# A two-mixer block on one core: the delta-rule merges eight turns later, with more zero products around them

## The chip, the cores and the metric

The kernel runs on one core of one Trainium2 chip. A core has a matmul engine (TensorE, PE in the profile, with its weight loads as PEld), a vector engine (DVE), an activation engine (ACT), a general-purpose engine (POOL), DMA queues fed from SyncE (SP), an on-chip memory (SBUF) and the matmul's accumulators (PSUM). Every engine works through its own list of instructions in order and meets the others at semaphores. The metric is the device time of one execution in microseconds.

## The reference

Three blocks follow each other on 256 tokens of width 1024, in float32. The first holds gated feed-forwards, a Mamba-2 mixer and a windowed attention. The last holds two mixers that read the same normalised input and a feed-forward with 16384 small experts. The change lies in the two mixers, which the reference computes so:

```
q = rms_norm(c_q, g_cq) @ w_uq          # 8 heads of 96
k_nope = rms_norm(c_kv) @ w_uk ; v = rms_norm(c_kv) @ w_uv
o = softmax(mask(q k^T * scale)) v ; o = rms_norm(o, g_attn_out)      # mixer 1

def rwkv7_step(state, inp):             # mixer 2, 256 steps, 8 heads of 64
    sk = einsum('bhij,bhj->bhi', state, kk_t)
    state = state * w_t - sk * (kk_t * a_t) + v_t * k_t
    y = einsum('bhij,bhj->bhi', state, r_t)
y = (group_norm(y) * ln_x_w + ln_x_b + bonus) * g
h = h + concat(o, y) @ w_o
```

## The kernel before, in words

Products of float32 matrices are made of three products of rounded halves: `mm3` (L153 to L155) multiplies low by high, high by low and high by high. Weights arrive by DMA as `wraw`; L93 (ACT) rounds them to `whi` and L99 (DVE or POOL) leaves the rest as `wlo`.

All of both mixers stands in `mixers`, as two generators that `run` steps in turn, one step of each per turn; a scheduler then sets every engine's list from the order in which this code records instructions. `weave(gens, lag)` starts one more generator every `lag` turns and steps all that live.

`rwkv` solves the delta rule in chunks of 64 steps. For each of four groups n of (chunk, head) pairs `gram` makes the triangular matrices; `base` inverts their 16 by 16 blocks by substitution on DVE (L1061, L1062) and writes X (L1074 on DVE, L1076 on ACT). Six empty turns follow (L1215). Then `merge(n)` joins the blocks at two levels: a zero product by `K.warm` (L77: a 256-column product of a zero tile with itself, into the bank that the next product overwrites), X times Lo on PE (L1088), a mask on DVE (L1091), another zero product, a product with Wt (L1097), a subtraction on DVE (L1099). After that `recur` runs four chunks c in order: state times AR (L1121, not for c = 0), MV (L1123), X times MV (L1129), VS (L1131 on ACT, L1132 on DVE), the state's update (L1139, L1153 to L1156) and the outputs `py` (L1147, L1148). After c = 1 and after c = 3 one half of the tokens is finished (`finish`): copies (L1170, ACT), mean and square (L1171 to L1176, DVE and ACT), nine small DVE operations of an inverse root (L168 to L176), a gate product (L1180, PE), two passes on POOL (L1184, L1185), four on DVE (L1186 to L1189), transposes (L1195, PE) and the split into bhi (L1202, ACT) and blo (L1203, DVE).

`mla` is the attention: `queries(m)`, m = 0 to 3, multiplies cqh and cql with 18 products each; `by_token` makes keys and values (kb); sums of squares are L1267; eight heads follow. Their output po is squared (L1410, ACT), summed (L1411, DVE), scaled by an inverse root (small DVE operations L168 to L176 again, named rsm) into ay (L1419, DVE), transposed (L1426, PE) and split into ahi (L1432, ACT) and alo (L1433, DVE). The output projection has 96 products of ahi and alo, then, once both generators have ended, 96 of bhi and blo; L264 (DVE) adds to h.

In the changed kernel every line past L1214 has one more in its number (L1426 is L1427).

Of the kernel before, what the change touches and what calls it, by code (L numbers as in the profile page):

```python
# [23 lines left out]
def weave(gens, lag=1):  # L24

    live, t = [], 0
    gens = list(gens)
    while gens or live:
        if gens and t % lag == 0:
            live.append(gens.pop(0))  # L30
        for g in list(live):
            if next(g, live) is live:
                live.remove(g)
        t += 1
        yield
# [765 lines left out]
def mixers(K, h, P, W, pool):  # L801
# [83 lines left out]
    def prep_k(m):  # L885
        ns = slice(2 * m, 2 * m + 2)
        ps = K.bank()
        for j in range(2):
            for st in range(2):
                for e, p in enumerate(halves):  # L890
                    K.bcast(kks, st, 4 * m + 2 * j + e, 64, ps[p, j * T + st * 128:j * T + (st + 1) * 128])
        kkn = tile_([128, 2, T], F32, name="kkn", tag="kkn")
        for j in range(2):
            n = 2 * m + j
            V.scalar_tensor_tensor(kkn[:, j], kT[:, n], P["kk"][:, n:n + 1], ps[:, j * T:(j + 1) * T], OP.mult, OP.mult)
        dp = Dp[:, 8 * m:8 * m + 8].rearrange("p (n c) j -> p n c j", c=4)
        di = Di[:, 8 * m:8 * m + 8].rearrange("p (n c) j -> p n c j", c=4)
        V.tensor_tensor(AR[:, ns, :, 0:64], chunked(kkn), dp[:, :, :, 0:64], OP.mult)
        V.tensor_mul(kkn, kkn, ra[:, ns])
        for j in range(2):  # L900
            n = 2 * m + j
            A.activation(ra[:, n], ra[:, n], AF.Identity, scale=P["ka"][:, n:n + 1], bias=ka1[:, n:n + 1])
        for e, p in enumerate(halves):
            V.tensor_tensor(BK[p, ns, :, 64 * e:64 * e + 64], chunked(kkn)[p], di[p], OP.mult)
        V.tensor_mul(kT[:, ns], ra[:, ns], kT[:, ns])
        for e, p in enumerate(halves):
            V.tensor_tensor(BK[p, ns, :, 64 - 64 * e:128 - 64 * e], chunked(kT[:, ns])[p], di[p], OP.mult)

    def prep_r(m):
        ns = slice(2 * m, 2 * m + 2)  # L910
        dp = Dp[:, 8 * m:8 * m + 8].rearrange("p (n c) j -> p n c j", c=4)
        V.tensor_tensor(AR[:, ns, :, 64:128], chunked(rT[:, ns]), dp[:, :, :, 1:65], OP.mult)
        for j in range(2):
            n = 2 * m + j
            V.scalar_tensor_tensor(rT[:, n], rT[:, n], P["rk"][:, n:n + 1], kT[:, n], OP.mult, OP.mult)
# [34 lines left out]
    ps = pair(2)  # L950
# [4 lines left out]
    ps = pair(3)  # L955
    kk_norm(1, sqs)
    shifted(ps, 3, 6, [rT[:, 0], rT[:, 1]])
    ps = pair(4)
# [64 lines left out]
    def gram(n):  # L1023

        s = slice(4 * n, 4 * n + 4)
        pgs = [K.bank(), K.bank()]
        for c in range(4):
            for e, p in enumerate(halves):
                TE.matmul(pgs[e][:, c * 128:(c + 1) * 128], BK[p, n, c], AR[p, n, c], start=True, stop=True)
        for e in range(2):  # L1030
            V.tensor_tensor(GM[e][:, s], pgs[e].rearrange("p (a b) -> p a b", b=128), gm, OP.mult)
        yield
        pts, pl = [K.bank(), K.bank()], K.bank()
        for c in range(4):
            for e, p in enumerate(halves):
                TE.transpose(pts[e][:, c * 64:c * 64 + 64], BK[p, n, c], ident[p, p])
        for c in range(4):
            for e, p in enumerate(halves):
                TE.matmul(pl[p, c * 64:c * 64 + 64], AR[p, n, c, 0:64], BK[p, n, c, 64 * e:64 * e + 64], start=True, stop=True)
        for e, hb, q in quads:  # L1040
            V.tensor_tensor(D16[q, s], GM[e][q, s, 32 * hb:32 * hb + 32], b16[q], OP.mult)
        yield
        for e in range(2):
            A.activation(BKt[:, n, e], b4(pts[e]), AF.Copy)
        A.activation(Lo[:, s], b4(pl), AF.Copy)
        yield

    def base():

        Tr = tile_([128, 16, 32], F32, name="Tr", tag="ry", bufs=2)  # L1050
        UX = tile_([128, 2, 256], F32, name="UX", tag="rsq")
        U, Y = (UX[:, i].rearrange("p (c i) -> p c i", i=16) for i in range(2))
        G.memset(UX[:, 1], 0.0)
        G.memset(UX[:, 1, 0:256:17], 1.0)
        dv = D16.rearrange("p b (s j) -> p j s b", s=2)
        V.transpose(Tr, dv)
        yield
        V.tensor_tensor(U, Tr[:, :, 0:16], Tr[:, :, 16:32], OP.add)
        for j in range(15, 0, -1):
            t = tile_([128, 64], F32, name="bt", tag="bt", bufs=2)[:, :j * (16 - j)].rearrange("p (c i) -> p c i", i=j)  # L1060
            V.tensor_tensor(t, U[:, j:j + 1, 0:j].to_broadcast([128, 16 - j, j]), Y[:, j:, j:j + 1].to_broadcast([128, 16 - j, j]), OP.mult)  # L1061
            V.tensor_tensor(Y[:, j:, 0:j], Y[:, j:, 0:j], t, OP.subtract)  # L1062
            if j % 4 == 1:
                yield
        m = P["b16"][:, 32:34]
        A.activation(Tr[:, :, 0:16], Y, AF.Copy, scale=m[:, 0:1])
        V.tensor_scalar(Tr[:, :, 16:32], Y, m[:, 1:2], None, OP.mult)
        yield
        V.transpose(dv, Tr)
        yield  # L1070
        for e, hb, q in quads:
            dst = X[q, :, 32 * hb:32 * hb + 32]
            if e:
                V.tensor_copy(dst, D16[q])  # L1074
            else:
                A.activation(dst, D16[q], AF.Copy)  # L1076
        yield

    def merge(n):

        s = slice(4 * n, 4 * n + 4)
        for lv in range(2):
            V.transpose(XT[:, s], X[:, s])
            ps = K.bank()
            K.warm(ps, 1)
            for c in range(4):
                for p in halves:
                    TE.matmul(ps[p, c * 64:c * 64 + 64], Lo[p, 4 * n + c], X[p, 4 * n + c], start=True, stop=True)  # L1088
            yield
            Wt = tile_([128, 4, 64], F32, name="Wt", tag="Wt", bufs=2)  # L1090
            V.tensor_tensor(Wt, b4(ps), um(lv), OP.mult)  # L1091
            yield
            ps = K.bank()
            K.warm(ps, 1)
            for c in range(4):
                for p in halves:
                    TE.matmul(ps[p, c * 64:c * 64 + 64], XT[p, 4 * n + c], Wt[p, c], start=True, stop=True)  # L1097
            yield
            V.tensor_tensor(X[:, s], X[:, s], b4(ps), OP.subtract)  # L1099
            yield  # L1100
# [106 lines left out]
    def rwkv():  # L1207
        for i in range(4):
            yield
            if i == 0:  # L1210
                prep_k(1)
                prep_r(1)
        yield from weave((gram(n) for n in range(4)), 2)
        yield from base()  # L1214
        for _ in range(6):  # L1215
            yield
        yield from weave((merge(n) for n in range(4)), 1)
        while MV is None:
            yield
        r = recur()  # L1220
        for _ in r:
            if todo and next(todo[0], todo) is todo:
                todo.pop(0)
            yield
        while todo:
            if next(todo[0], todo) is todo:
                todo.pop(0)
            yield
# [206 lines left out]

    pq, blko = None, K.stream(W["wo"])
    run((rwkv(), 1), (mla(), 1))
    run(K.proj_half(blko, 1, bhi, blo, h))

# [545 lines left out]
```

## Time and profile before

| what | value |
|---|---|
| time before, median of 3 runs | 2120.3 us (2118.93 to 2123.44) |
| the profiled execution's own time, its span | 2126.33 us, 2124.6 us |
| PE, PEld | busy 2081.3 us (98%), 1961.8 us (92%) |
| DVE, ACT, POOL | busy 1553.1 us (73%), 1098.0 us (52%), 127.1 us (6%) |
| mean granted clock of PE | 0.986 of full speed |

The profile is one execution, with microseconds counted from the span's start. PEclk is the clock that PE was granted, as a share of 2.4 GHz: 1.00 is 2.4 and 0.50 is 1.2 GHz. A row of the timeline gives start, length, engine, line, operation, output and inputs; in brackets how long the engine had been idle before, and what released it. The two mixers lie near the middle of the span, and their merges, recurrence and heads from about 1150 to 1262 us.

### The profile page before, as it was taken

The page shows a single profiled execution, that of the slowest core. Times are in us where ns is not written, and L with a number is a line of the kernel's source. Part 1 is how long each engine was busy: PE and PEld are TensorE (multiplying, and loading weights), DVE is VectorE, ACT ScalarE, POOL GpSimd, SP SyncE. Part 2 cuts the span into 40 slices and gives each one's busy share as a digit, 9 for nine tenths or more (in the row PEclk, how much of TensorE's full clock was granted, in tenths as well). Part 3 has the DMA queues.
Part 4 walks back from the last instruction along what each step waited for, and adds up shares of the span by engine and source line. Part 5 has one row for each costly group of instructions (what it writes and reads, how often), then busy time and mean ns, then how long its engine had stood idle before and what let it go on. Part 6 is the DMA issues. An engine that isn't in the chain of part 4 may idle for free.

```text
span 2124.6 us, 40996 instructions
## 1 busy us (share of the span) xinstructions
PE 2081.3 (98%) x16546; PEld 1961.8 (92%) x16546; DVE 1553.1 (73%) x2950; ACT 1098.0 (52%) x1903; POOL 127.1 (6%) x94
## 2 busy tenths in 40 slices
PE   8999999999999999999999998999999999999999
PEld 8999998999999998999998778999999998888887
DVE  6665977876576658776578678997888896555555
ACT  5444678554454445654454346553444444444444
POOL 0000000000000000000001105850000000000000
PEclk9999999999999999999998899999999999999999
DMA  6655443577555553555533126442444445555554
GB/s 209 191 188 176 160 149 109 168 204 204 184 184 180 184 183 110 170 190 188 189 130 100 51 66 223 151 159 96 156 159 158 158 160 169 191 192 191 188 189 149
DMA packets 98282, 348.15 MB, mean 164 GB/s; under 512 B 11084, under 2 KB 13997, under 8 KB 97837
## 3 DMA queue, kind: packets, MB, share of 16 engines
q1 hardware_dynamic: 98092, 345.54, 49.7%
q8 instruction: 130, 2.13, 0.4%
q14 instruction: 60, 0.48, 0.1%
HBM read 344.05 MB, written 1.44 MB: 163 GB/s over the span
## 4 chain that ended last, share of the span: by engine, by line
PE 88%; DVE 9%; ACT 1%; issue 1%; DMA 0%; POOL 0%; SPq 0%; DVEq 0%; ACTq 0%
PE ps L153 20%; PE ps L154 20%; PE ps L155 20%; PE pacc L1691 6%; PE pacc L1693 6%; PE pacc L1692 5%; DVE wlo L99 2%; PE ps L1638 2%; DVE cv L433 1%; ACT whi L93 1%; PE wo L153 1%; PE wo L155 1%; PE wo L154 1%; PE ps L199 1%; DVE eq L1539 0%
## 5 line engine op out<-in xcount | busy, mean ns | idle before, releaser
L99 DVE TENSOR_TENSOR wlo<-wraw,whi 128x1024 fp32r<-128x1024 f32 x611 | 755.5, 1237 | 298.1 <-ACT whi L93 295.5
L93 ACT ACTIVATE whi<-wraw 128x1024 fp32r<-128x1024 f32 x644 | 676.8, 1053 | 374.1 <-PE ps L155 211.3
L153 PE MATMUL ps<-xhi,wlo 128*128 128x256 f32 x1960 | 555.3, 283 | 8.5 <-DVE wlo L124 6.8
L154 PE MATMUL ps<-xlo,whi 128*128 128x256 f32 x1960 | 551.8, 282 | 2.0 <-DVE xlo L182 1.2
L155 PE MATMUL ps<-xhi,whi 128*128 128x256 f32 x1960 | 549.2, 280 | 0.0
L153 PEld LDWEIGHTS ps<-xhi,wlo 128*128 128x128 f32 x1960 | 369.9, 189 | 14.1 <-DVE wlo L124 6.8
L154 PEld LDWEIGHTS ps<-xlo,whi 128*128 128x128 f32 x1960 | 369.5, 189 | 4.8 <-DVE xlo L182 4.5
L155 PEld LDWEIGHTS ps<-xhi,whi 128*128 128x128 f32 x1960 | 369.2, 188 | 0.2
L153 PE MATMUL ps<-phi,wlo 128*128 128x256 f32 x1024 | 294.7, 288 | 10.3 <-ACT phi L1512 4.2
L154 PE MATMUL ps<-plo,whi 128*128 128x256 f32 x1024 | 289.2, 282 | 0.6 <-DVE plo L1513 0.6
L155 PE MATMUL ps<-phi,whi 128*128 128x256 f32 x1024 | 288.2, 282 | 0.0
L153 PEld LDWEIGHTS ps<-phi,wlo 128*128 128x128 f32 x1024 | 194.9, 191 | 12.0 <-ACT phi L1512 4.3
L1691 PE MATMUL pacc<-whi,cl 128*128 128x512 f32 x512 | 203.6, 398 | 1.5 <-DVE cl L1683 1.5
L1693 PE MATMUL pacc<-whi,ch 128*128 128x512 f32 x512 | 200.5, 392 | 0.0
L1692 PE MATMUL pacc<-wlo,ch 128*128 128x512 f32 x512 | 199.2, 389 | 0.0
L153 PE MATMUL ps<-ghi,wlo 128*128 128x256 f32 x704 | 197.9, 281 | 0.0
L154 PE MATMUL ps<-glo,whi 128*128 128x256 f32 x704 | 197.6, 281 | 0.0
L155 PE MATMUL ps<-ghi,whi 128*128 128x256 f32 x704 | 197.5, 280 | 0.0
L154 PEld LDWEIGHTS ps<-plo,whi 128*128 128x128 f32 x1024 | 195.1, 191 | 0.9 <-DVE plo L1513 0.9
L155 PEld LDWEIGHTS ps<-phi,whi 128*128 128x128 f32 x1024 | 194.2, 190 | 0.0
L154 PEld LDWEIGHTS ps<-glo,whi 128*128 128x128 f32 x704 | 132.7, 188 | 0.0
L155 PEld LDWEIGHTS ps<-ghi,whi 128*128 128x128 f32 x704 | 132.4, 188 | 0.0
(537 smaller groups left out, 3101.4 us busy)
## 6 DMA issues: line engine op xcount, KB each, us to landing
wraw<-in_w SPq DMA_DIRECT2D x262, 512.0 KB, 3.7
wraw<-in_p_u SPq DMA_DIRECT2D x128, 512.0 KB, 3.7
wraw<-in_p_v SPq DMA_DIRECT2D x128, 512.0 KB, 3.6
wraw<-in_m_win SPq DMA_DIRECT2D x40, 512.0 KB, 4.2
wraw<-in_x_win SPq DMA_DIRECT2D x20, 512.0 KB, 3.6
wraw<-in_m_wout SPq DMA_DIRECT2D x16, 512.0 KB, 3.8
wraw<-in_p_wpq SPq DMA_DIRECT2D x16, 512.0 KB, 4.4
wraw<-in_a_wq SPq DMA_DIRECT2D x8, 512.0 KB, 3.6
```

The lines of the kernel that those rows point to most:

```text
L93: nc.scalar.activation(hi, w, AF.Copy)
L99: (nc.vector if lo_eng == "dve" else nc.gpsimd).tensor_sub(lo, w, hi.bitcast(F32))
L153: nc.tensor.matmul(ps, wl, xh, start=first, stop=False)
L154: nc.tensor.matmul(ps, wh, xl, start=False, stop=False)
L155: nc.tensor.matmul(ps, wh, xh, start=False, stop=last)
L199: self.nc.tensor.matmul(out, r[:, c:c + 1].to_broadcast([128, n]), self.ident, start=True, stop=True)
L433: V.scalar_tensor_tensor(y, xp[:, j, q:q + T], w[:, c, q:q + 1], y, OP.mult, OP.add)
L1638: TE.matmul(ps[:, q * 128:(q + 1) * 128], oh[:, q // 2 * 2, :, q % 2], og[:, q // 2 * 3 + z, :, q % 2], start=z == 2, stop=z == 0)
L1691: TE.matmul(o, cl[:, t], vh[:, f], start=False, stop=False)
L1692: TE.matmul(o, ch[:, t], vl[:, f], start=False, stop=False)
L1693: TE.matmul(o, ch[:, t], vh[:, f], start=False, stop=last)
```

## The change

Each of the two zero products of a merge becomes two; the wait before the merges grows from 6 empty turns to 14; and eight more zero products are recorded right before the merges. That is 16 + 8 = 24 zero products more.

```diff
@@ -1082,7 +1082,7 @@
             V.transpose(XT[:, s], X[:, s])
             ps = K.bank()
-            K.warm(ps, 1)
+            K.warm(ps, 2)
@@ -1091,7 +1091,7 @@
             ps = K.bank()
-            K.warm(ps, 1)
+            K.warm(ps, 2)
@@ -1212,8 +1212,9 @@
         yield from base()
-        for _ in range(6):
-            yield
+        for _ in range(14):
+            yield
+        K.warm(K.bank(), 8)
         yield from weave((merge(n) for n in range(4)), 1)
```

Since `mla` takes a step in every turn, what it records meanwhile stands ahead of the merges. The lists of the engines differ only inside the two mixers. **First place:** PE's list before, from the sums of the query inputs to the first product of the merges (L77 zero product, L1088 X times Lo, cqh and cql query products).

```order
L1267 MATMUL ps<-ones,sqc 128x1 x2
...
L155 MATMUL ps<-cqh,whi 128x256
L77 LDWEIGHTS zero
L77 MATMUL ps<-zero 128x256
L153 MATMUL ps<-cqh,wlo 128x256
L1088 MATMUL ps<-X,Lo 64x64 x8
```

The same place in PE's list of the changed kernel:

```order
L1268 MATMUL ps<-ones,sqc 128x1 x2
...
L1268 MATMUL pk<-ones,AW 128x1 x2
...
L1268 MATMUL pq<-ones,cv 128x1 x2
L153 MATMUL kb<-whi,ckl 128x512
L1282 MATMUL ps<-cst,AW 128x32 x2
...
L155 MATMUL kb<-whi,ckh 128x512
L153 MATMUL ps<-cqh,wlo 128x256
L154 MATMUL ps<-cql,whi 128x256
L155 MATMUL ps<-cqh,whi 128x256
L77 LDWEIGHTS zero
L77 MATMUL ps<-zero 128x256
```

The rest of the first two queries' products, their sums (pk, pq) and the twelve products of the keys (kb) moved ahead of the first L1088, which stands behind ten zero products. **Second place:** PE's list before, from the last head's output po to the transposes of ay.

```order
L635 MATMUL po<-vt,asT 128x64
L77 LDWEIGHTS zero
...
L1129 MATMUL ps<-MV,X 64x64 x8
L1148 MATMUL py<-VS,GM_13361 64x64
...
L1148 MATMUL py<-VS,GM_13362 64x64
L1426 MATMUL ps<-cst,ay 128x128 x8
L153 MATMUL ps<-ahi,wlo 128x256
L1180 MATMUL ps<-px,sg 128x512
```

And in the changed kernel:

```order
L635 MATMUL po<-vt,asT 128x64
L77 LDWEIGHTS zero
...
L1180 MATMUL ps<-px,sg 128x512
L1121 MATMUL ps<-S,AR 64x64 x8
...
L1129 MATMUL ps<-MV,X 64x64 x8
L1427 MATMUL ps<-cst,ay 128x128 x8
L77 LDWEIGHTS zero
...
L1139 MATMUL ps<-VS,BK 64x64 x8
```

The L1129 ahead of the transposes is that of c = 3 before and that of c = 2 in the changed kernel, where a state update, a whole chunk and the second `finish` follow behind them. **Third place:** the entry to the projection's second half, in PE's list before.

```order
L153 MATMUL ps<-ahi,wlo 128x256
L154 MATMUL ps<-alo,whi 128x256
L155 MATMUL ps<-ahi,whi 128x256
L153 MATMUL ps<-bhi,wlo 128x256
L154 MATMUL ps<-blo,whi 128x256
L155 MATMUL ps<-bhi,whi 128x256
```

And in the changed kernel, from the last output of the recurrence on (24 products of ahi and alo stand between it and L1180):

```order
L1148 MATMUL py<-VS,GM_13362 64x64
L153 MATMUL ps<-ahi,wlo 128x256
...
L155 MATMUL ps<-ahi,whi 128x256
L1180 MATMUL ps<-px,sg 128x512
L1195 MATMUL ps<-cst,ry 128x128 x4
L153 MATMUL ps<-bhi,wlo 128x256 x3
L154 MATMUL ps<-blo,whi 128x256
```

Before, L1180 and L1195 of that half stood among the 96 products of ahi, which all came after the last py; now 24 of the 96 are left behind it.

## Rows read from the trace of the kernel before

**Rows 1.** The page's chain that ended last, share of the span by engine
```profile
PE 88%; DVE 9%; ACT 1%; issue 1%; DMA 0%; POOL 0%; SPq 0%; DVEq 0%; ACTq 0%
```

**Rows 2.** Idle time of PE by line: engine, line, waited for, us, times, longest
```profile
PE ps L1426 <- DVE ay L1419: 3.1, 1, 3.1
...
PE ps L1088 <- ACT X L1076: 2.3, 1, 2.3
...
PE ps L1088 <- DVE X L1074: 1.0, 1, 1.0
...
PE ps L1267 <- DVE UX L1062: 0.7, 1, 0.7
...
PE py L1148 <- ACT VS L1131: 0.5, 1, 0.5
PE ps L153 <- ACT ahi L1432: 0.5, 1, 0.5
```

**Rows 3.** Windows of 5 us: busy us by engine (instructions), PE's clock, DMA, GB/s
```profile
1150.00:1155.00 5.00, 2.06 (x16) 1.61 (x14) 4.51 (x12) 3.20 (x6) 1.59 (x1) 1.00 0.27 93
1155.00:1160.00 5.00, 4.03 (x31) 3.43 (x32) 4.77 (x8) 2.34 (x5) 2.58 (x2) 0.51 0.33 108
1160.00:1165.00 5.00, 5.00 (x43) 4.53 (x41) 0.85 (x2) 0.00 (x0) 0.00 (x0) 0.50 0.32 105
1180.00:1185.00 5.00, 5.00 (x62) 3.98 (x61) 1.91 (x6) 0.00 (x0) 0.00 (x0) 0.76 0.00 0
1245.00:1250.00 5.00, 4.30 (x13) 2.87 (x14) 4.43 (x14) 2.11 (x7) 2.31 (x2) 0.50 0.00 0
1250.00:1255.00 5.00, 5.00 (x41) 5.00 (x41) 4.53 (x13) 1.71 (x3) 0.00 (x0) 0.93 0.06 16
```

**Rows 4.** Timeline, PE in the merges: start us, us, engine, line, out<-in, tile, count
```profile
1170.77 1.12 PE L1088 MATMUL ps<-X,Lo 64*64 64x64 f32 x16
...
1184.03 0.68 PE L1088 MATMUL ps<-X,Lo 64*64 64x64 f32 x16
...
1200.34 0.38 PE L77 MATMUL ps<-zero 128*128 128x256 bf16 x2
```

**Rows 5.** Timeline, the attention output's chain, and two small operations of DVE
```profile
1223.35 1.04 POOL L1184 TENSOR_TENSOR rsq<-vtk,bon 128x512 f32<-128x512 f32 x1 [19.51 <-DVE rm L1176]
...
1223.44 0.97 DVE L168 TENSOR_SCALAR rsla<-rm 128x8 f32<-128x8 f32 x1
...
1236.46 0.60 ACT L1410 ACTIVATE msq<-po 128x512 f32<-128x512 f32 x1 [0.84 <-PE po L635]
...
1237.09 0.69 DVE L1411 TENSOR_REDUCE mu__13378<-msq 128x8 f32<-128x512 f32 x1 [0.31 <-ACT msq L1410]
...
1238.02 0.17 DVE L168 TENSOR_SCALAR rsma<-mu__13378 128x16 f32<-128x16 f32 x1
...
1244.50 1.29 DVE L1419 TENSOR_TENSOR ay<-po,mnm 128x512 f32<-128x512 f32 x2
```

**Rows 6.** Timeline, the last half of the recurrence's output, to the projection
```profile
1242.14 0.38 ACT L1170 ACTIVATE ry<-py 128x256 f32<-128x256 f32 x1 [1.86 <-PE py L1148]
...
1242.55 0.69 DVE L1171 TENSOR_REDUCE rm<-ry 128x8 f32<-128x512 f32 x1 [2.86 <-ACT ry L1170]
...
1244.29 0.63 ACT L1175 ACTIVATE rsq<-ry 128x512 f32<-128x512 f32 x1 [1.76 <-DVE mnm L176]
...
1248.05 1.91 PE L1180 MATMUL ps<-px,sg 128*128 128x512 f32 x2
...
1254.99 1.22 DVE L99 TENSOR_TENSOR wlo<-wraw,whi 128x1024 fp32r<-128x1024 f32 x1
...
1257.13 0.60 PE L1195 MATMUL ps<-cst,ry 128*128 128x128 f32 x4
...
1258.39 0.69 DVE L1203 TENSOR_TENSOR blo<-ps,bhi 128x512 fp32r<-128x512 f32 x1 [0.16 <-ACT bhi L1202]
...
1261.77 0.28 PE L153 MATMUL ps<-bhi,wlo 128*128 128x256 f32 x1
```

## The prediction, written before the changed kernel ran

> **What bounds the kernel now.** I read the page's chain that ended last first: matmuls are 88% of it [rows 1], so time is lost where PE waits or where PE runs slowly. Next I read PE's waits by line, for the two mixers alone, since the edit changes no list outside them. Of these waits three stand where the merges begin: 0.7 for the sums L1267, 2.3 and 1.0 for X before L1088, together 4.0 us; and three at the attention's end: 0.5, 3.1 and 0.5, together 4.1 us [rows 2]. Last I read windows of 5 us for the granted clock. It is 1.00 up to 1155 and 0.51 and 0.50 right after, although PE is busy for 5.00 of 5 us from 1160 on; the window from 1180 has a mean of 0.76 [rows 3]. A mean of 0.51 means 4.9 us at half, so the fall lies at about 1155.1; 0.76 means 2.4 us at half, so the return lies at about 1182.4. The merges and the products beside them thus ran for 27.3 us at 1.2 GHz. It happens again at the attention's end: 0.50 from 1245 to 1250, 0.93 after [rows 3].
>
> What half clock costs is read from one step at both levels: 16 products of L1088 took 1.12 us at half and 0.68 at full [rows 4]. So 1 - 0.68/1.12 = 0.39 of the PE time at half is loss.
>
> **The change, part by part.**
>
> *a, the clock through the merges.* Now PE reaches the merges after the queries' and keys' products, when X has long been written, so the waits of 2.3 and 1.0 us go. What may be late instead is the work of ACT and DVE on the queries; I find by following the two lists about 2 us of waiting there, before the zero products, in two pieces shorter than the one before. I take it that the clock then stays full. Of the 27.3 us at half 1.0 was waiting; 26.3 x 0.39 = 10.3 us come back. Bounds: 0 to 10.3; taken 10.3, because the clock was 1.00 until the waits came [rows 3].
>
> If the clock should fall here too, two rows give the price: as in the merges of before, half for as long as these last, 10.3 us; or as at the attention's end, where about 5 us of busy PE ran at half before it returned [rows 3], 5.0 x 0.39 = 2.0 us. The Trainium skill, page "TensorE: Matmul & The Clock Gate", Part 1, says that half rate is the default and that activity of the array releases it; by that the smaller price would hold, and a would be -8.3 after a fall, the sum +10.8. The rows of the merges do not agree with it: 5.00 of 5 us busy at 0.50 [rows 3]; by them a would be 0 after a fall, the sum +19.1.
>
> *b, 24 zero products.* Two take 0.38 us from first start to last end at full clock [rows 4], and one 0.28 like every 256-column product (the last row of [rows 6]); so one more costs 0.10: 24 x 0.10 = 2.4 us, all on PE. At half clock twice that, 4.8. Some could fill waits, down to 0; taken 2.4.
>
> *c, the first waits.* I count 3.3 us of PE waiting between the old and the new start of the merges against 4.0 before, so -0.7. But the merges' DVE steps now meet a weight split that POOL does. What POOL does to a short DVE operation: L168 took 0.97 beside L1184 and 0.17 alone, 0.8 lost [rows 5]. I take 1.2, one and a half times that. Sum +0.5, bounds -0.7 to +1.7.
>
> *d, the transposes of ay.* In the second place of the lists L1427 stands behind L1129 of c = 2, soon after the last po, and DVE's list now mixes the first half's finish into the chain from po to ay. Lengths as measured [rows 5, 6]: two L1410 1.20; the second L1411 0.69; three passes of finish (L1171, L1173, L1176) at 0.69 make 2.07; two operations half as wide 0.7; about 15 small ones at 0.2 make 3.0; the first half of L1419 0.65. That is 8.3 us. L1184 and L1185 now run in it; I let three small operations lose 0.8 each, 2.4: 10.7 us. Beside it PE has L1180 (1.91 at half [rows 6], so about 1.0 at full), four zero products, L1121 and L1129 (0.68 each, as L1088 at full [rows 4]): 2.7 us. It waits 8.0 where 4.1 were lost: +3.9. Lowest: none of finish and no POOL, 6.2 - 2.7 - 4.1 = -0.6; highest +6, if finish's operations lose as much again. The loss by half clock behind this wait I take to be as before.
>
> *e, the first projection products* now follow alo pieces between which DVE runs finish's four passes of 0.69. Before, PE waited 0.5 there [rows 2]; I take +1.0, bounds 0 to 2.
>
> *f, the wait before bhi.* In before 96 products of ahi lie behind the last py. A window at nearly full clock holds 41 products in 5.00 us [rows 3], 0.122 each, 11.7 us in all. The chain to blo ran from 1242.14 (L1170) to 1258.39 + 0.69 = 1259.08, that is 16.9 us, and the first product of bhi started at 1261.77 [rows 6]: 2.7 us of reserve. Now the third place of the lists leaves 24 products, 2.9 us, and L1180, 1.0. The chain, with lengths as measured [rows 5, 6]: L1170 0.38, seven DVE passes at 0.69 make 4.83, L1175 0.63, ten small operations 2.0, L1195 0.60, bhi 0.60 (as L1410), handing over 0.5: 9.5 us. In DVE's list one addition to h (0.69) and one weight split (1.22, L99) stand in between, +1.9; POOL's two passes +2.4 as in d: 13.8 us. PE is busy for 2.9 + 1.0 + 0.6 of it (L1195 is PE's own), so it waits 9.3 us. Before it waited 0. Bounds: the bare chain 9.5 - 4.5 = 5.0; the chain as long as before 16.9 - 4.5 = 12.4.
>
> *g, the clock behind that wait.* At the attention's end a wait of 3.1 us went with half clock: 4.30 us of busy PE in one window at 0.50, and 0.7 us more in the next at 0.93 [rows 3], 5.0 x 0.39 = 2.0 us. A wait of 9.3 us should do the same: +2.0, bounds 0 to 4.
>
> *Where the rest hides.* The query and key products moved forward are PE work that PE does anyway, at no cost but the clock's. POOL's list is the same; SP's loads keep their order but for one small table (iota), moved; the share of DMA in the stretch is 0.33 at most [rows 3], so nothing is priced.
>
> **Sum:** -10.3 + 2.4 + 0.5 + 3.9 + 1.0 + 9.3 + 2.0 = +8.8 us. Against the profiled execution's own 2126.33 this is 2135.1. That execution lies 6.0 above the median of the runs; the same sum on the median of 2120.3 gives **2129.1 us**, which I predict. Its own range, from single terms at their bounds, is 2123 to 2136.
>
> **The rivals.**
>
> *The clock falls all the same.* For it: the fall in before came after waits of 2.3 and 1.0 us, and about 2 us of waiting are still there, ahead of the merges. Against it: they come in shorter pieces, and ten zero products follow at once. If it falls and stays at half as long as in before, a is 0: the sum is 8.8 + 10.3 = +19.1 us, 2139.4. If it falls and returns as at the attention's end, the sum is 8.8 + 2.0 = +10.8 us, 2131.1. (The second is what the page's rule on activity would give.)
>
> *The late chains run bare.* For it: d and f contain holds by POOL and foreign DVE passes that depend on the meeting of the moment, and the scheduler's order puts urgent ones early. Then d is 0, e 0.5, f 5.0, g 1.5, and the sum is -10.3 + 2.4 + 0.5 + 0 + 0.5 + 5.0 + 1.5 = -0.4, that is 2119.9: no change. Against it: all the foreign passes stand in DVE's list ahead of the step that PE waits for, and the list is in order.
>
> *Faster: the late waits are paid already.* The recurrence starts some 3 us earlier, since the merges run at full clock, and before's own path to bhi has 2.7 us to spare. If PE reaches the last py and the transposes of ay so late, by all the work that now stands ahead of them, that the chains have time to end, d to g are 0 and the sum is -10.3 + 2.4 + 0.5 = -7.4: 2112.9. It ends faster than before, whatever the single waits are, as long as d to g stay under 7.4 us together. Against it: only 3.9 us of other PE work stand between the last py and the products of bhi, and no order of arrival makes the bare 9.5 us shorter.
>
> **How the numbers follow.** About 0.2%, 4.2 us, is what a measurement of this kernel can tell from no change. Chances: the forecast 0.48, of which 0.03 fall within 4.2 us; the clock rival 0.12 (0.07 at 2139.4, 0.05 at 2131.1); bare chains 0.22; the faster rival 0.18. So slower 0.45 + 0.12 = 0.57, same 0.03 + 0.22 = 0.25, faster 0.18. The range of 8 in 10 goes from 2114.0, which leaves out somewhat more than half of the faster rival (0.11), to 2138.0, which leaves out the upper clock case (0.07) and a little of the forecast's tail (0.02).
>
> **What would show it.** Right: a granted clock of 1.00 in the 30 us after the first zero products; a wait of PE for ay of about 8 us at L1427 and one of about 9 us for bhi or blo before the second half of the projection, with 0.50 after it; zero products 0.10 apart. Wrong in a: windows of 0.50 through the merges. Wrong in f: a wait for bhi under 5 us, or ahi products that still run when blo is written. Wrong in d: L1427 released within 4 us of the last product ahead of it. If all late waits are under 2 us, the forecast fails and the kernel is faster.

## The result, and the profile after

The changed kernel took 2139.8 us (median of 4 runs, 2138.0 to 2145.2) against 2121.9 for the kernel before on the same chip: a ratio of 1.0089 (95% interval 1.0069 to 1.0110), some 19 us slower. The prediction had the sign right; 2139.8 lies 1.8 us above its range and the loss is twice the 8.8 us that it summed.

The chain that ended last, on the page of the changed kernel (shares of the span by engine), answers [rows 1]:

```profile
PE 87%; DVE 9%; ACT 2%; issue 1%; DMA 0%; POOL 0%; SPq 0%; DVEq 0%; ACTq 0%
```

PE still sets the time. Its waits in the two mixers (engine, line, what it waited for, us in total, times, longest) answer [rows 2]:

```profile
PE ps L1195 <- DVE ry L1189: 8.6, 1, 8.6
...
PE ps L1427 <- DVE ay L1420: 5.5, 1, 5.5
...
PE pq L1268 <- ACT cv L1354: 1.8, 1, 1.8
...
PE ps L153 <- ACT bhi L1202: 0.7, 1, 0.7
PE ps L1268 <- DVE UX L1062: 0.7, 1, 0.7
```

The waits of 2.3 and 1.0 us for X are gone; one of 1.8 us for ACT's cv has come. The wait for ay has grown from 3.1 to 5.5 us, and 8.6 + 0.7 us are new ahead of bhi, where PE did not wait before. Windows of 5 us in the same kernel (busy time of PE, PEld, DVE, ACT and POOL, then PE's clock, DMA share and GB/s) answer [rows 3]:

```profile
1155.00:1160.00 5.00, 4.19 (x18) 3.69 (x18) 4.72 (x9) 2.70 (x6) 2.36 (x1) 0.55 0.31 108
1160.00:1165.00 5.00, 5.00 (x20) 4.61 (x21) 1.67 (x4) 0.93 (x2) 1.80 (x1) 0.50 0.55 188
1165.00:1170.00 5.00, 5.00 (x21) 3.87 (x19) 2.90 (x12) 2.14 (x3) 0.15 (x1) 0.58 0.06 22
1215.00:1220.00 5.00, 5.00 (x53) 3.88 (x51) 0.06 (x1) 0.49 (x1) 0.00 (x0) 1.00 0.00 0
1220.00:1225.00 5.00, 5.00 (x24) 3.10 (x24) 2.90 (x6) 1.85 (x4) 0.00 (x0) 0.54 0.00 0
1245.00:1250.00 5.00, 5.00 (x31) 4.32 (x31) 1.63 (x4) 0.78 (x3) 0.00 (x0) 0.50 0.00 0
1260.00:1265.00 5.00, 5.00 (x29) 4.27 (x28) 1.96 (x4) 0.77 (x2) 0.00 (x0) 0.64 0.32 107
1270.00:1275.00 5.00, 0.00 (x0) 0.00 (x0) 4.66 (x12) 0.00 (x0) 2.32 (x2) 0.66 0.31 105
1280.00:1285.00 5.00, 5.00 (x25) 4.99 (x24) 0.10 (x1) 0.00 (x0) 0.00 (x0) 0.50 0.00 0
```

Read the clock beside the first busy figure. At the merges half clock ends at about 1169 instead of 1182. But PE is busy for 5.00 of 5 us from 1215 to 1225, and the clock falls there to a mean of 0.54. It comes back at about 1227.2 and falls again in the wait for ay, from about 1230.6 to 1251.1. It falls once more in the window from 1260, is back from about 1268.2 to 1271.6, falls inside the wait for L1195 and stays at 0.50 to about 1285.2, through the first products of bhi. Where it fell is seen product by product (start, length, output, inputs, count):

```profile
1216.70 0.32 PE L1147 MATMUL py<-S,AR 64*64 64x64 f32 x2
...
1220.03 0.27 PE L1148 MATMUL py<-VS,GM 128*64 128x64 f32 x1
...
1220.29 0.41 PE L1147 MATMUL py<-S,AR 64*64 64x64 f32 x2
...
1220.64 0.47 PE L1148 MATMUL py<-VS,GM 128*64 128x64 f32 x2
```

A pair of output products lasts 0.32 us at full clock, the pairs at 1220.29 and 1220.64 last 0.41 and 0.47: the clock fell in the middle of the 32 products of py of c = 1, which ran back to back without a wait. It fell again in those of c = 3, at 1261.3.

How PE's time is spent, worked out from the timeline of each trace: from the start of one PE instruction to that of the next, less the waits, from the first sums L1267 to the last product of bhi, in us.

| | wait | zero | merges | queries, keys, sums | py | ahi | bhi | rest | all |
|---|---|---|---|---|---|---|---|---|---|
| before, the trace read for the prediction | 8.1 | 7.4 | 14.9 | 25.5 | 12.7 | 12.8 | 11.1 | 29.6 | 122.1 |
| before, a second trace (e5) | 8.0 | 6.9 | 13.2 | 23.9 | 12.1 | 12.0 | 11.1 | 29.5 | 116.7 |
| changed | 15.9 | 10.1 | 10.0 | 25.3 | 16.4 | 17.4 | 14.0 | 33.9 | 142.9 |
| changed, a second trace (e1) | 16.7 | 9.4 | 10.0 | 24.2 | 16.0 | 14.3 | 13.0 | 30.7 | 134.4 |

Between the second traces 17.7 us are lost: 8.7 of waiting, 2.5 of zero products, and 9.3 of py, ahi, bhi and the rest, the same work in a stretch with more half clock; 3.2 come back in the merges.

### The profile page after: what moved, and what is told of

It is laid out like the page before. It is cut to its first block, busy times and chain, and to the rows that moved or that the text cites. A ratio compares the mean times of both kernels' runs of the same rounds, so it can differ in the third digit from the quotient of the medians.

```text
span 2143.4 us, 41049 instructions
## 1 busy us (share of the span) xinstructions
PE 2091.4 (98%) x16570; PEld 1969.8 (92%) x16570; DVE 1556.0 (73%) x2950; ACT 1097.7 (51%) x1903; POOL 127.6 (6%) x94
## 4 chain that ended last, share of the span: by engine, by line
PE 87%; DVE 9%; ACT 2%; issue 1%; DMA 0%; POOL 0%; SPq 0%; DVEq 0%; ACTq 0%
PE ps L153 20%; PE ps L154 20%; PE ps L155 19%; PE pacc L1692 6%; PE pacc L1694 6%; PE pacc L1693 5%; DVE wlo L99 2%; PE ps L1639 2%; DVE cv L433 1%; ACT whi L93 1%; PE wo L153 1%; DVE eq L1540 1%; PE wo L155 1%; PE wo L154 1%; PE ps L199 1%
## 5 line engine op out<-in xcount | busy, mean ns | idle before, releaser
L99 DVE TENSOR_TENSOR wlo<-wraw,whi 128x1024 fp32r<-128x1024 f32 x611 | 757.2, 1240 | 296.4 <-ACT whi L93 294.2
L93 ACT ACTIVATE whi<-wraw 128x1024 fp32r<-128x1024 f32 x644 | 676.8, 1053 | 385.7 <-PE ps L155 219.7
L155 PE MATMUL ps<-xhi,whi 128*128 128x256 f32 x1960 | 548.9, 280 | 0.0
L155 PEld LDWEIGHTS ps<-xhi,whi 128*128 128x128 f32 x1960 | 368.7, 188 | 0.3
L155 PE MATMUL ps<-phi,whi 128*128 128x256 f32 x1024 | 287.2, 281 | 0.0
L155 PE MATMUL ps<-ghi,whi 128*128 128x256 f32 x704 | 197.5, 281 | 0.0
L155 PEld LDWEIGHTS ps<-phi,whi 128*128 128x128 f32 x1024 | 193.2, 189 | 0.0
L155 PEld LDWEIGHTS ps<-ghi,whi 128*128 128x128 f32 x704 | 132.4, 188 | 0.0
```

The lines of the kernel that those rows point to most:

```text
L93: nc.scalar.activation(hi, w, AF.Copy)
L99: (nc.vector if lo_eng == "dve" else nc.gpsimd).tensor_sub(lo, w, hi.bitcast(F32))
L155: nc.tensor.matmul(ps, wh, xh, start=False, stop=last)
```

## The experiments

**Is it the order or the zero products?** e1 is the changed kernel again; e2 has its 14 turns without the zero products, e3 the zero products with 6 turns.

```diff
 # e2, against the changed kernel
-            K.warm(ps, 2)          # both places in merge
+            K.warm(ps, 1)
-        K.warm(K.bank(), 8)
 # e3, against the changed kernel
-        for _ in range(14):
+        for _ in range(6):
```

> The changed kernel once more, for a second trace. Theory 1 (the new order loses time: waits for ay and bhi, and half clock wherever the 32 products of py run in one block): 2136 to 2142 us again, a wait for ay of 5 to 6 us, one for bhi of 9 to 10 us, and the clock falls again inside the blocks of py of c = 1 and c = 3, while PE has no wait there. Rival (the clock fell there by chance, or behind waits alone): the same waits, but the falls at other places, and a time that moves by 5 us or more.

> Only the 14 empty turns, without the 24 more zero products. Theory 1 (the order): 2.4 us less than the changed kernel, 2135 to 2139 us, with both late waits as long (about 5.5 and 9.3 us). Rival (the zero products make the loss, as work or by what they do to the clock): 2120 to 2126 us.

> Only the 24 more zero products, with the 6 empty turns of the kernel before; ten of them now stand in PE's list before the first product of X. Theory 1: 24 x 0.10 = 2.4 us more than before, 2123 to 2126 us, if the clock falls at the first merge as before; 2112 to 2116 us if the ten fill the wait of 2.3 us there and the clock stays full. Rival (the zero products make the loss): 2134 us or more.

Measured: e1 2140.0 us (ratio to before 1.0087, 1.0068 to 1.0107), with the same two waits (5.6 and 8.8). Its clock fell inside the last output block again (1255.1 in 1251.6 to 1256.1), but behind the first one (1224.4, in the wait for ay), so theory 1 held for three blocks of four in two traces (those of c = 2 ran at half already). e2 2136.5 (1.0067, 1.0047 to 1.0087), waits of 5.5 and 8.8. e3 2120.2 (0.9988, 0.9978 to 0.9999): no slower at all, and in neither of the two ranges that theory 1 gave. The order carries the loss; the zero products cost some 3 us on top of it (by the medians) and nothing without it, since ten of them ran inside the first wait for X, which went from 2.3 to 1.4 us.

**The late order.** e4 moves the transposes of ay and the projection back by the same 8 turns; e8 leaves the transposes of ay, but moves the projection and the last L1195 so that some 80 products stand behind the last py.

```diff
 # e4, in mla, ahead of the transposes of ay
-        for _ in range(2):
+        for _ in range(10):
             yield
 # e8, in mla ahead of proj_half, and in finish ahead of the transposes
+        for _ in range(8):
+            yield
-        for _ in range(3):
+        for _ in range(6 if st else 3):
```

> The changed kernel with 8 empty turns more in the attention's generator, ahead of the transposes of ay, so that these and the projection come after the recurrence's last outputs again. Theory 1: the wait before bhi (9.3 us) and the half clock behind it go; what is left is the shorter half clock through the merges (about -5 us) and the zero products (+2.4): 2117 to 2123 us. Rival (the loss comes from the merges or the zero products, not from the late order): 2135 us or more.

> The changed kernel with the projection's first half 8 turns later in the attention's generator, and the last transposes of the recurrence's output 3 turns later, so that some 80 products instead of 24 stand between the last output and these transposes. Theory 1 (the wait before bhi is that of a chain of about 13 us with too little to cover it): the wait for the transposes goes from 8.8 to 1 to 4 us, the time to 2131 to 2137 us, since PE now waits more inside chunk c = 3. Rival (the wait is set by what DVE must do for the projection first, and moves with it): 8 us or more of waiting there, 2138 us or more.

Measured: e4 2129.2 us (1.0041, 1.0029 to 1.0053), halfway: the wait for ay went, but PE waited 9.0 us in two pieces for the transposes L1195 and 2.4 us ahead of an output product L1147; that this is because what stands ahead of them ran earlier too is argued, not tested. The expected 2117 to 2123 was missed. e8 2132.5 (1.0063, 1.0042 to 1.0084), inside theory 1's range, though the wait was less short than it said:

```profile
PE ps L1427 <- DVE ay L1420: 5.5, 1, 5.5
PE ps L1195 <- DVE ry L1189: 5.5, 1, 5.5
```

5.5 us in place of 8.8 ahead of L1195, so the reserve behind the last output is a cause of that wait, not the only one. By the ratios e8 takes 5 us less than e1, but the two intervals overlap.

**The clock in the output products.** e6 puts zero products between them.

```diff
+            pw = K.bank()
             for n in range(4):
+                K.warm(pw, 4 if c else 0)
                 for e, p in enumerate(halves):
                     o = py[e][o0, n * 64:n * 64 + 64]
```

> The changed kernel with 4 zero products ahead of each group of 8 output products of c = 1, 2, 3 (48 more, 4.8 us of PE at full clock). Theory 1 (a block of nothing but the 64-column output products takes the clock down): no fall inside these blocks, only behind the two late waits; what that gives back, 5 to 8 us, pays for the zero products: 2134 to 2141 us. Rival (the clock falls for another reason, such as the coming wait): the falls stay where they were, 2143 to 2146 us.

Measured: 2135.3 us (1.0076, 1.0052 to 1.0100), in theory 1's range. In its trace zero products take 16.4 us, 7.0 more than in e1, py 13.5 instead of 16.0 and ahi 12.0 instead of 14.3; the ratio is no worse than e1's 1.0087 (the intervals overlap, so no gain in time is shown either). Windows of e6 that hold the outputs of c = 1 (1211.7 to 1217.5) and of c = 3 (1249.0 to 1254.9), and the wait that follows:

```profile
1210.00:1215.00 5.00, 5.00 (x52) 3.47 (x51) 0.00 (x0) 0.37 (x1) 0.00 (x0) 1.00 0.00 0
1215.00:1220.00 5.00, 5.00 (x47) 3.38 (x47) 2.27 (x5) 1.76 (x4) 0.00 (x0) 1.00 0.00 0
1250.00:1255.00 5.00, 5.00 (x39) 3.42 (x38) 0.99 (x1) 0.49 (x2) 0.00 (x0) 1.00 0.32 108
1260.00:1265.00 5.00, 0.00 (x0) 0.00 (x0) 4.59 (x12) 0.00 (x0) 1.80 (x1) 0.75 0.28 105
```

The clock is 1.00 through both blocks and falls only inside the waits that follow, at 1225.0 and 1262.5; the block of c = 2 (1231.5 to 1237.5), at whose start it came back, saw no fall either. So, in this one trace, zero products between the parts of the blocks keep the clock up to the waits. The other traces bear it out: in the changed kernel, e1, e2, e4, e8 and e11 to e13 twelve unbroken blocks of 32 began at full clock, and it fell inside nine of them.

**What the kernel before loses at the merges.** e5 is the kernel before once more.

> The kernel before once more, for a second trace. Theory 1 (the 27.3 us at half clock through the merges, on which the gain of 10.3 us was reckoned, were more than an ordinary run has): the clock falls at about 1155 again but comes back by 1165 to 1176, and the time is 2116 to 2121 us. Rival (they are what this order always does): half clock until about 1182 and 2124 us or more.

Measured: 2116.9 us. Windows of this second trace:

```profile
1150.00:1155.00 5.00, 1.88 (x18) 1.63 (x19) 4.82 (x8) 4.64 (x9) 2.32 (x2) 0.83 0.23 73
1155.00:1160.00 5.00, 5.00 (x35) 4.42 (x33) 3.21 (x5) 0.07 (x1) 1.85 (x1) 0.50 0.42 139
1165.00:1170.00 5.00, 5.00 (x45) 4.22 (x45) 3.53 (x10) 1.33 (x2) 1.80 (x1) 0.50 0.00 0
1170.00:1175.00 5.00, 5.00 (x73) 3.70 (x73) 3.08 (x12) 0.82 (x2) 0.00 (x0) 0.97 0.30 108
```

The clock fell inside the waits (at about 1153.3) and was back at about 1170.3: 17.1 us of half clock, 16.9 of them busy, against 27.3 and 26.3 in the trace on which the gain was reckoned. The runs of this kernel that stood beside the others fall into two groups, 2115 to 2121 us at a mean clock of 0.990 to 0.992 (one at 0.988) and 2123 to 2128 at 0.985 to 0.989; the profiled execution of 2126.33 was of the second. Theory 1 holds: those 27.3 us did not belong to the order alone.

**Does the wait take the clock down at the merges?** e7, e9 and e11 fill the waits with zero products; e10 fills the late one too.

```diff
 # e7 (40) and e9 (20), in rwkv of the kernel before
+        K.warm(K.bank(), 20)
         yield from weave((merge(n) for n in range(4)), 1)
 # e10: e9, and in mla ahead of the transposes of ay
+        K.warm(K.bank(), 28)
 # e11, in queries of the changed kernel, ahead of its sums
+            if m == 0:
+                K.warm(K.bank(), 18)
```

> The kernel before with 40 zero products ahead of the merges, 4.0 us, in place of the two longest waits there (3.3 us). Theory 1 (the waits take the clock down at the merges): the fall at 1155 does not come, 2110 to 2116 us. Rival (the zero products do not count for the clock, or the mix of small merge products takes it down by itself): the clock falls all the same, 2119 to 2124 us.

> The kernel before with 20 zero products ahead of the merges, which PE runs in the first wait for X (2.3 us). Theory 1 (a wait takes the clock down there): no fall at the merges, or one that lasts 10 us or less, and 2 to 6 us less than before, 2112 to 2116 us. Rival (the small products of the merges take it down by themselves): a fall of 14 us or more after the wait has gone, and the time of before or 1 us more.

> The same, with 28 zero products more ahead of the transposes of ay, some of which fall among the last output products. Theory 1 (a block of output products, and a wait behind it, take the clock down; zero products between keep it): the fall at 1235 to 1243 goes, the 28 cost 1 to 2 us of PE outside its wait, the time is that of the kernel with 20, or 1 to 2 us less: 2111 to 2115 us. Rival (the zero products do not keep the clock): the fall is there and the time 1 to 3 us more than with 20.

> The changed kernel with 18 zero products ahead of the sums that wait 1.8 us for ACT in the first stretch. Theory 1 (that wait takes the clock down ahead of the merges): no fall around 1150 to 1170, or a later and shorter one, and 1 to 4 us less than the changed kernel, 2135 to 2139 us; the falls in the output products stay. Rival (the clock falls there for another reason): a fall of 10 us or more and 2140 to 2142 us.

Measured: e7 2118.9 us (1.0001, 0.9986 to 1.0016), e9 2122.9 (1.0010, 0.9997 to 1.0023), e11 2145.4 (1.0107, 1.0084 to 1.0131). None gained, and all three lie above theory 1's ranges, for a reason that no theory had: the scheduler moved the next sums forward. PE in e9, by its timeline and windows:

```profile
1152.69 0.51 PE L77 MATMUL ps<-zero 128*128 128x256 bf16 x3
...
1155.37 0.32 PE L1088 MATMUL ps<-X,Lo 64*64 64x64 f32 x2 [0.16 <-ACT X L1076]
...
1161.19 0.59 PE L1268 MATMUL ps<-ones,sqc 128*128 128x1 f32 x2 [3.43 <-DVE sqc L971]
```

```profile
1155.00:1160.00 5.00, 1.65 (x20) 1.02 (x18) 4.82 (x8) 2.98 (x6) 3.17 (x2) 1.00 0.33 108
1160.00:1165.00 5.00, 3.81 (x23) 3.35 (x25) 2.44 (x9) 0.00 (x0) 0.06 (x1) 0.53 0.31 105
```

21 zero products fill the wait for X (0.16 us is left of 2.3), and the clock stays at 1.00 past 1155, by which it had fallen in both traces of the kernel before. But sums that had stood inside the first product with Wt (L1097) now come before it and wait 3.4 us for DVE, and there the clock falls, at 1160.3, for 20 us. e7 had 5.2 us of such a wait, with the fall inside it at 1155.2, e11 4.4 and its fall at 1160.6. So the fall went with the wait and moved with it; what an order without any wait would give was not reached. e10, 2124.4 (1.0021, 1.0008 to 1.0033), breaks up the last outputs (14 and 14 in a row) and shortens the wait for ay from 3.1 to 1.2 us, both at once:

```profile
1240.00:1245.00 5.00, 4.50 (x36) 3.21 (x36) 1.86 (x8) 0.87 (x3) 0.00 (x0) 1.00 0.00 0
1245.00:1250.00 5.00, 2.91 (x15) 1.84 (x15) 4.95 (x12) 2.32 (x7) 2.31 (x2) 1.00 0.02 3
```

Here the kernel before has half clock [rows 3]; in e10 the clock is at 1.00 from 1176.9 to the end of the projection. Yet the time is 1.5 us above e9's by the medians, as the rival had it, though the fall that the rival needed is gone: what the 28 products return, they seem to cost.

**A step or a slope?** e12 and e13 are the changed kernel with 8 and 10 turns.

> The changed kernel with 8 empty turns in place of 14, all its zero products kept. In PE's list 18 query products more stand ahead of the merges than with 6 turns, and the late part is in the old order: the transposes of ay behind the last output, some 88 products between that and bhi. Theory 1 (the late order makes the loss): a wait for ay of 3 to 4 us, none before bhi over 2 us, and 2116 to 2121 us. Rival (merges begun later cost by themselves): 2126 us or more.

> The same with 10 turns: here the transposes of ay stand ahead of the last chunk's products, and some 35 projection products are left behind the last output. Theory 1: about 4 us of PE for these against a chain of about 13, so a wait of 5 to 8 us before bhi, a fall in the last output block, and 2126 to 2134 us. Rival (the loss grows with the turns evenly): 2 turns are a quarter of 8, so 2121 to 2125 us for 8 turns and 2126 to 2130 for 10.

Measured: e12 2121.9 us (1.0010, 0.9995 to 1.0026), e13 2128.7 (1.0042, 1.0023 to 1.0062). Six runs of e13 lie at 2122 to 2126 us, with a mean clock of 0.991 or 0.992, and six at 2132 to 2137 with 0.985 to 0.987; its trace is of the first six, and its median stands between the two. In e12 there is no wait for ay or bhi over 1 us, but two windows around its output blocks read:

```profile
1210.00:1215.00 5.00, 5.00 (x25) 4.82 (x25) 2.43 (x8) 1.96 (x7) 0.00 (x0) 0.54 0.00 0
1230.00:1235.00 5.00, 4.21 (x46) 3.12 (x44) 3.83 (x15) 1.13 (x3) 0.00 (x0) 0.50 0.00 0
```

4.1 us of waiting in all, half of what the kernel before has, and yet no faster: what the waits gave went to half clock (py 15.0 us against 12.1) and to the zero products (10.7 against 6.9). e13 waits 5.1 us ahead of L1195, as expected, but the fall expected in its last output block did not come; it came inside that wait, at 1252.2. e12 lies in the slope's range and 1 us above theory 1's, e13 in both: the waits speak for a step, the times do not decide, and this stays open.

## Why the prediction was wrong, point by point

By the second traces the sum of +8.8 missed in three places. The gain of a was 3.2 us instead of 10.3, the half clock of the late stretch cost 9.3 instead of 2.0, and all waits together (c to f) grew by 8.7 instead of 14.7. The first two put some 14 us on the time, the third takes 6 off; with 0.5 in the smaller terms that makes the 17.7 of the table.

**a, the clock through the merges (-10.3): wrong in size and in what it was counted against.** The clock did fall, in the 1.8 us wait for cv or just behind it: the rival "the clock falls all the same" happened, and it returned after 10 to 14 us. The merges took 10.0 us instead of 14.9 in the trace that was read, but only 3.2 less than in e5. A gain that one execution's own half clock offers was carried over to the median of the runs, which is 6 us faster, and by their mean clock most of those runs have less of it.

**d and g, half clock behind the late waits (0 and +2.0): the step that failed.** It put the fall at 1240 down to the wait of 3.1 us, and so took it to be as before. In the kernel before the clock fell at 1240.4, 1.7 us ahead of that wait, inside the output products of c = 3. The window that holds it, and the pairs on both sides of the fall:

```profile
1240.00:1245.00 5.00, 2.10 (x12) 1.43 (x12) 2.38 (x8) 1.29 (x3) 0.00 (x0) 0.54 0.00 0
```

```profile
1240.16 0.33 PE L1148 MATMUL py<-VS,GM 128*64 128x64 f32 x2
1240.42 0.47 PE L1147 MATMUL py<-S,AR 64*64 64x64 f32 x2
```

The prediction took its price from the two windows behind this one. (In e5 the fall came 0.2 us behind the start of the wait.) In the old order the outputs of c = 1 and 2 are broken up by the heads' work, with 22 and 23 products in a row in the trace, and no fall came inside those two blocks in any of the six traces with that order (the two of the kernel before, e3, e7, e9, e10). In the new order three blocks of 32 run alone. From 1200 us to the last product of bhi the clock was at half for 10.2 and 6.8 us in the two traces of the kernel before, and for 47.8 and 30.7 us in those of the changed kernel. Py, ahi, bhi and the rest cost 9.3 us more (second traces), and e6 shows that the blocks bring part of it about; how much falls to the blocks and how much to the longer waits was not separated.

**d, the wait for ay (+3.9): too large.** From the last po (1222.4) to the transposes (1232.85) it is 10.5 us, close to the 10.7 reckoned, but at half clock PE's own work beside it lasted 5.0 us instead of 2.7. Wait 5.5 us instead of 8.0. e (+1.0) did not appear in PE's waits.

**f, the wait before bhi (+9.3): right in size, 8.6 + 0.7, by another path.** The chain of the last finish, in the changed kernel:

```profile
1262.64 0.38 ACT L1170 ACTIVATE ry<-py 128x256 f32<-128x256 f32 x1 [0.42 <-PE py L1148]
...
1263.98 0.69 DVE L1173 TENSOR_TENSOR ry<-ry,rm 128x512 f32<-128x512 f32 x1
...
1267.82 0.77 PE L1180 MATMUL ps<-px,sg 128*128 128x512 f32 x1
...
1268.06 1.06 ACT L93 ACTIVATE whi<-wraw 128x1024 fp32r<-128x1024 f32 x1 [5.04 <-PE ps L155]
...
1269.02 0.61 ACT L1175 ACTIVATE rsq<-ry 128x512 f32<-128x512 f32 x1
...
1276.82 0.69 DVE L1189 TENSOR_TENSOR ry<-ry,ps 128x512 f32<-128x512 f32 x1
...
1277.66 0.66 PE L1195 MATMUL ps<-cst,ry 128*128 128x128 f32 x2 [8.63 <-DVE ry L1189]
```

The square L1175 was ready to run at 1264.7, when L1173 ended, but stands behind L93 in ACT's list, and L93 waits for the last of the 24 products (L155), until 1268. So, other than the working had it, the chain stood still beside those products: 15.0 us to L1195 instead of about 12, and 6.4 us of cover, mostly at half clock, instead of 3.9. Two errors of about 3 us cancelled, which is luck. Beside POOL's two passes the small operations L169 and L171 took 0.91 and 1.12 us where the others take 0.17, so some 1.7 us went there of the 2.4 reckoned.

**b, the zero products (+2.4): right**, 2.5 and 2.7 in the two pairs of traces; **c (+0.5)**: the first waits fell by 1.5 us, and PE had no wait in the merges, so no hold by POOL showed.

**The rivals.** Bare chains and the faster case are refuted by the waits. The price of the clock rival, 2139.4, is what was measured, but by luck, for another reason: most of the half clock stands late, not in the merges.

## What to carry to other kernels

Shifting one of two interleaved generators by eight turns moved their later meetings too, here some 60 and 100 us behind the first merges: read the end of the stretch in the new order, not only the place that is edited. Before a gain in clock is priced from one profile, compare that execution's time with the median; if it is slower, part of the gain is already in the median. A PE that is always busy is not a PE at full clock: look at what it runs where the clock falls. Of all versions e3, the zero products with the old turns, was the fastest: 0.12% (0.01 to 0.22) under the kernel before, less than the 0.2% that the prediction named as the least that can be told from no change.

## What was not expected of the hardware

The granted clock fell from 2.4 to 1.2 GHz while PE ran nothing but output products of 64 columns back to back, with no wait (nine of the twelve unbroken blocks that began at full clock, over all traces), and did not fall in the same blocks with four 256-column zero products ahead of each eight (e6, one trace). What in these products brings it about was not tried. It also returned in the midst of unbroken work, in the kernel before after 27 us in one execution and 17 in another, so how long half clock lasts is not read off an order.
